# A masked copy as eight memory-to-memory transfers: the order in which two DMA queues go through the rows

## The chip, the cores and the metric

The kernel runs on one core of a Trainium2 chip. The metric is the device time of one launch in microseconds (us); a lower time is better. Of the core's engines only the two that issue the large transfers matter here, SyncE (SP) and ScalarE (ACT), with the 16 DMA engines that carry out what they issue. VectorE (DVE) and TensorE (PE) do a small test beside the transfers.

## The reference

```
batch, seq, hidden, capacity = 16, 1024, 512, 256
x: (16, 1024, 512) float32;  token_positions: (16, 1024) int, drawn from 0 to 255

mask = token_positions < capacity
return (x * mask[..., np.newaxis]).astype(np.float32)
```

A token whose position is at or beyond the capacity has its row of 512 numbers set to zero; every other row is returned as it is. With these inputs every position is below 256, so the output equals `x`.

## The kernel before, in words

The 16,384 rows of 2 KB are seen as 128 parts of 128 consecutive rows, one part for each partition number `p`. A part is 256 KB of consecutive memory, in `x` and in `out` alike, and part `p + 1` begins where part `p` ends. In the code `x_r` and `out_r` are this view, with the indices (p, n, d).

The kernel copies first and asks afterwards. Eight DMAs (L79) move `x` straight to `out` inside the device's memory, 4 MB each. DMA number `k` takes rows `k*16` to `k*16 + 15` of every part, which is block `k` of eight blocks of 32 KB in each of the 128 parts. The even `k` are issued by SP and the odd `k` by ACT, so each engine's queue holds four DMAs and works them off in the order of issue. All eight add to one semaphore, `s_copy`, and nothing waits between them. The list `early` gathers these DMAs, and a few lines of list handling move them to the front of the program, ahead of the start-up barrier of the engines. Ahead of ACT's four stands one small load (L72) of the positions to `tp`.

While the copies run, DVE builds the mask `keep` from `tp` in four operations (L103 to L115), sums it (L119), PE adds the sums over the partitions (L123), and DVE compares the total with the number of rows (L125). The answer, `drop_i`, says whether any token has to be dropped. SP, ACT and DVE read it and branch on it (L133, `nc.If(drop)`). Within the branch the kernel would load all rows to SBUF, multiply them by the mask and store them; with these inputs the branch isn't taken. At the end GpSimd (POOL) waits until `s_copy` has all eight DMAs, sets the semaphores back, and the program is over.

So the end of the program is set by the DMA that lands last. The order in which the blocks are copied is fixed by the loop over `k` and by the two queues, and no other step of the program reads what they write.

Of the kernel before, what the change touches and what calls it, by code (L numbers as in the profile page):

```python
# [1 line left out]

# [4 lines left out]


@with_exitstack
def kernel(  # L10
    ctx: ExitStack,
    tc: tile.TileContext,
    x: bass.AP,
    token_positions: bass.AP,
    capacity: bass.AP,
    out: bass.AP,
):
    nc = tc.nc
    P = nc.NUM_PARTITIONS
    fp32 = mybir.dt.float32  # L20
    i32 = mybir.dt.int32
    Alu = mybir.AluOpType

    x_f = x.flatten_outer_dims()
    out_f = out.flatten_outer_dims()
    N, D = x_f.shape
    n_per_p = N // P
    cap = float(int(capacity))
    x_r = x_f.rearrange("(p n) d -> p n d", p=P)
    out_r = out_f.rearrange("(p n) d -> p n d", p=P)  # L30
    tp_i32 = token_positions.rearrange("b s -> (b s)").bitcast(i32)

    sp = nc.sync
    act = nc.scalar
    ve = nc.vector
    pe = nc.tensor
    gp = nc.gpsimd


    tc.close()  # L40
    tc.compile()  # L41

    def sbuf(name, shape, dtype):
        return ctx.enter_context(nc.sbuf_tensor(name, shape, dtype)).ap()

    tp = sbuf("tp", [P, 2 * n_per_p], i32)
    ge = sbuf("ge", [P, n_per_p], fp32)
    lt = sbuf("lt", [P, n_per_p], fp32)
    low = sbuf("low", [P, n_per_p], fp32)
    keep = sbuf("keep", [P, n_per_p], fp32)  # L50
    kept = sbuf("kept", [P, 1], fp32)
    ones = sbuf("ones", [P, 1], fp32)
    drop_i = sbuf("drop_i", [1, 1], i32)
    total = ctx.enter_context(nc.psum_tensor("total", [1, 1], fp32)).ap()
    F = 16
    NBUF = 2
    n_fix = n_per_p // F
    xts = [sbuf(f"xt{b}", [P, F, D], fp32) for b in range(NBUF)]

    s_copy = nc.alloc_semaphore("s_copy")  # L60
    s_tp = nc.alloc_semaphore("s_tp")
    s_ve = nc.alloc_semaphore("s_ve")
    s_pe = nc.alloc_semaphore("s_pe")
    s_ld = [nc.alloc_semaphore(f"s_ld{b}") for b in range(NBUF)]
    s_mul = nc.alloc_semaphore("s_mul")
    s_st = [nc.alloc_semaphore(f"s_st{b}") for b in range(NBUF)]
    s_done = nc.alloc_semaphore("s_done")

    n_copy = 0
    early = []  # L70

    load_tp = act.dma_start(out=tp, in_=tp_i32.rearrange("(p w) -> p w", p=P))  # L72
    early.append(load_tp.then_inc(s_tp, 16).ins)

    C = 16
    for k in range(n_per_p // C):
        ins = (sp, act)[k % 2].dma_start(  # L79
            out=out_r[:, k * C : (k + 1) * C, :], in_=x_r[:, k * C : (k + 1) * C, :]  # L80
        ).then_inc(s_copy, 16)
        early.append(ins.ins)
        n_copy += 1


    home = nc.cur_bb.bb
    first_bb = nc.cur_f.blocks[0]
    first_sp = next(
        k for k, i in enumerate(first_bb.instructions) if i.engine == mybir.EngineType.SP
    )  # L90
    names = [i.name for i in early]
    home.instructions = [i for i in home.instructions if i.name not in names]
    first_bb.instructions = (
        first_bb.instructions[:first_sp] + early + first_bb.instructions[first_sp:]
    )

    lo = tp[:, 0 : 2 * n_per_p : 2]
    hi = tp[:, 1 : 2 * n_per_p : 2]


    ve.memset(ones, 1.0).then_inc(s_ve, 1)  # L101
    ve.wait_ge(s_tp, 16)
    ve.tensor_scalar(  # L103
        out=ge, in0=lo, scalar1=0.0, scalar2=None, op0=Alu.is_ge
    ).then_inc(s_ve, 1)
    ve.wait_ge(s_ve, 2)
    ve.scalar_tensor_tensor(  # L107
        out=lt, in0=lo, scalar=cap, in1=ge, op0=Alu.is_lt, op1=Alu.mult
    ).then_inc(s_ve, 1)
    ve.wait_ge(s_ve, 3)  # L110
    ve.scalar_tensor_tensor(  # L111
        out=low, in0=hi, scalar=0.0, in1=lt, op0=Alu.is_equal, op1=Alu.mult
    ).then_inc(s_ve, 1)
    ve.wait_ge(s_ve, 4)
    ve.scalar_tensor_tensor(  # L115
        out=keep, in0=hi, scalar=0.0, in1=low, op0=Alu.is_lt, op1=Alu.add
    ).then_inc(s_ve, 1)
    ve.wait_ge(s_ve, 5)
    ve.tensor_reduce(  # L119
        out=kept, in_=keep, axis=mybir.AxisListType.X, op=Alu.add  # L120
    ).then_inc(s_ve, 1)
    pe.wait_ge(s_ve, 6)
    pe.matmul(out=total, lhsT=ones, rhs=kept, start=True, stop=True).then_inc(s_pe, 1)  # L123
    ve.wait_ge(s_pe, 1)
    ve.tensor_scalar(  # L125
        out=drop_i, in0=total, scalar1=float(N) - 0.5, scalar2=None, op0=Alu.is_lt
    ).then_inc(s_ve, 1)


    for e in (sp, act, ve):  # L130
        e.wait_ge(s_ve, 7)
    ET = mybir.EngineType
    drop = nc.values_load(  # L133
        drop_i[0:1, 0:1],
        engines=[ET.SP, ET.Activation, ET.DVE],
        min_val=0,
        max_val=1,
        skip_runtime_bounds_check_because="a comparison gives 0 or 1",
    )
    with nc.If(drop):  # L140
        for u in range(n_fix):
            b = u % NBUF
            if u >= NBUF:
                sp.wait_ge(s_st[b], 16 * (u // NBUF))
            sp.dma_start(out=xts[b], in_=x_r[:, u * F : (u + 1) * F, :]).then_inc(s_ld[b], 16)
            ve.wait_ge(s_ld[b], 16 * (u // NBUF + 1))
            for j in range(F):
                c = u * F + j
                ve.tensor_scalar(
                    out=xts[b][:, j, :],  # L150
                    in0=xts[b][:, j, :],
                    scalar1=keep[:, c : c + 1],
                    scalar2=None,
                    op0=Alu.mult,
                ).then_inc(s_mul, 1)
            if u == 0:
                act.wait_ge(s_copy, 16 * n_copy)
            act.wait_ge(s_mul, (u + 1) * F)
            act.dma_start(out=out_r[:, u * F : (u + 1) * F, :], in_=xts[b]).then_inc(s_st[b], 16)
        for b in range(NBUF):  # L160
            act.wait_ge(s_st[b], 16 * (n_fix // NBUF))


    for e in (sp, act, ve):
        e.sem_inc(s_done, 1)
    gp.wait_ge(s_done, 3)
    own = [s_tp, s_ve, s_pe, *s_ld, s_mul, *s_st, s_done]
    ids = sorted(s.num for s in own)
    assert ids == list(range(ids[0], ids[-1] + 1))
    gp.sem_clear(range(ids[0], ids[-1] + 1))  # L170
    gp.wait_ge(s_copy, 16 * n_copy)
    gp.sem_inc(s_copy, -16 * n_copy)


# [1 line left out]
_INS = ['x', 'token_positions', 'capacity']  # L176
_OUTS = [((16, 1024, 512), 'float32')]

_NUMBERS = {'capacity': 256}


# [26 lines left out]
```

## Time and profile before

| | |
|---|---|
| median of 3 runs | 106.08 us (105.78 to 106.34) |
| the profiled execution, its own time | 106.19 us |
| its span, first to last instruction | 104.3 us |
| memory read, memory written | 33.69 MB, 33.55 MB |
| mean rate of the DMA engines over the span | 323 GB/s |
| DVE busy, PE busy | 1.5 us, 0.2 us |

The profile is of one execution, and its times count from the first instruction. Its DMA row is the mean busy share of the 16 DMA engines in 40 equal slices of the span, in tenths, and the row below it is what they moved. A copy from memory to memory counts once in that rate, and twice (read and written) in the memory's own line. `q1` and `q10` are the queues that SP and ACT fill. A packet is the piece that one DMA engine moves at a time. A window's rate counts each packet whole, so a short window is rough by a packet or two on each engine.

### The profile page before, as it was taken

The page shows a single profiled execution, that of the slowest core. Times are in us where ns is not written, and L with a number is a line of the kernel's source. Part 1 is how long each engine was busy: PE and PEld are TensorE (multiplying, and loading weights), DVE is VectorE, ACT ScalarE, POOL GpSimd, SP SyncE. Part 2 cuts the span into 40 slices and gives each one's busy share as a digit, 9 for nine tenths or more (in the row PEclk, how much of TensorE's full clock was granted, in tenths as well). Part 3 has the DMA queues.
Part 4 walks back from the last instruction along what each step waited for, and adds up shares of the span by engine and source line. Part 5 has one row for each costly group of instructions (what it writes and reads, how often), then busy time and mean ns, then how long its engine had stood idle before and what let it go on. Part 6 is the DMA issues. An engine that isn't in the chain of part 4 may idle for free. (4 is left out here: it accounts for less than half of the span.)

```text
span 104.3 us, 70 instructions
## 1 busy us (share of the span) xinstructions
PE 0.2 (0%) x2; PEld 0.1 (0%) x2; DVE 1.5 (1%) x7; POOL 0.2 (0%) x4
## 2 busy tenths in 40 slices
PE   0000000000000000000000000000000000000000
PEld 0000000000000000000000000000000000000000
DVE  0230000000000000000000000000000000000000
POOL 0000000000000000000000000000000000000000
DMA  8999989989989989999899997998997999989984
GB/s 251 402 352 302 339 280 339 339 302 352 339 289 390 314 276 377 289 327 352 289 364 327 302 377 239 377 377 289 352 327 276 377 327 314 390 276 327 364 277 163
DMA packets 1297, 33.69 MB, mean 323 GB/s; under 512 B 144, under 2 KB 272, under 8 KB 272
## 3 DMA queue, kind: packets, MB, share of 16 engines
q10 hardware_dynamic: 720, 16.91, 49.4%
q1 hardware_dynamic: 576, 16.78, 48.6%
q14 instruction: 1, 0.01, 0.0%
HBM read 33.69 MB, written 33.55 MB: 645 GB/s over the span
## 5 line engine op out<-in xcount | busy, mean ns | idle before, releaser
L107 DVE SCALAR_TENSOR_TENSOR lt<-tp,ge 128x128 f32<-128x128 int32 x1 | 0.3, 293 | 0.0
L111 DVE SCALAR_TENSOR_TENSOR low<-tp,lt 128x128 f32<-128x128 int32 x1 | 0.3, 291 | 0.0
L115 DVE SCALAR_TENSOR_TENSOR keep<-tp,low 128x128 f32<-128x128 int32 x1 | 0.3, 291 | 0.0
L119 DVE TENSOR_REDUCE kept<-keep 128x1 f32<-128x128 f32 x1 | 0.3, 286 | 0.0
L103 DVE TENSOR_SCALAR ge<-tp 128x128 f32<-128x128 int32 x1 | 0.2, 228 | 0.0
L123 PE MATMUL total<-kept,ones 128*1 128x1 f32 x2 | 0.2, 164 | 6.2 <-DVE kept L119 6.2
L125 DVE TENSOR_SCALAR drop_i<-total 1x1 int32<-1x1 f32 x1 | 0.1, 145 | 0.3 <-PE total L123 0.3
L101 DVE MEMSET ones<- 128x1 f32 x1 | 0.1, 59 | 4.6 <-PEq L41 4.6
L189 POOL MEMSET const-bfloat16-1.0<- 128x1 bf16 x1 | 0.1, 101 | 0.0
L189 POOL MEMSET const-uint8-127<- 128x1 uint8 x1 | 0.1, 101 | 0.0
L189 POOL MEMSET const-float32-0.0<- 128x1 f32 x1 | 0.1, 98 | 0.2 <-issue 0.2
L189 POOL MEMSET const-float32-1.0<- 128x1 f32 x1 | 0.1, 98 | 0.0
L123 PEld LDWEIGHTS total<-kept,ones 128*1 128x1 f32 x2 | 0.1, 80 | 6.2 <-DVE kept L119 6.2
## 6 DMA issues: line engine op xcount, KB each, us to landing
out_dram<-in_x_dram SPq DMA_DIRECT2D x4, 4096.0 KB, 62.2
out_dram<-in_x_dram ACTq DMA_DIRECT2D x4, 4096.0 KB, 68.1
tp<-in_token_positions_dram ACTq DMA_DIRECT2D x1, 128.0 KB, 2.1
```

The source lines that it names most:

```text
L101: ve.memset(ones, 1.0).then_inc(s_ve, 1)
L103: ve.tensor_scalar(out=ge, in0=lo, scalar1=0.0, scalar2=None, op0=Alu.is_ge).then_inc(s_ve, 1)
L107: ve.scalar_tensor_tensor(out=lt, in0=lo, scalar=cap, in1=ge, op0=Alu.is_lt, op1=Alu.mult).then_inc(s_ve, 1)
L111: ve.scalar_tensor_tensor(out=low, in0=hi, scalar=0.0, in1=lt, op0=Alu.is_equal, op1=Alu.mult).then_inc(s_ve, 1)
L115: ve.scalar_tensor_tensor(out=keep, in0=hi, scalar=0.0, in1=low, op0=Alu.is_lt, op1=Alu.add).then_inc(s_ve, 1)
L119: ve.tensor_reduce(out=kept, in_=keep, axis=mybir.AxisListType.X, op=Alu.add).then_inc(s_ve, 1)
L123: pe.matmul(out=total, lhsT=ones, rhs=kept, start=True, stop=True).then_inc(s_pe, 1)
L125: ve.tensor_scalar(out=drop_i, in0=total, scalar1=float(N) - 0.5, scalar2=None, op0=Alu.is_lt).then_inc(s_ve, 1)
L189: nc = _bacc.Bacc("TRN2", target_bir_lowering=False, num_devices=1)
```

## The change

The eight DMAs stay as they are in size, number, issuing engine and order of issue; the block that each takes is another. SP's four take blocks 0, 1, 2, 3 instead of 0, 2, 4, 6. ACT's four take blocks 7, 6, 5, 4 instead of 1, 3, 5, 7. Everything after the loop stands two lines lower and is unchanged.

```diff
     C = 16
-    for k in range(n_per_p // C):
+    n = n_per_p // C
+    for k in range(n):
+        j = k // 2 if k % 2 == 0 else n - 1 - k // 2
         ins = (sp, act)[k % 2].dma_start(
-            out=out_r[:, k * C : (k + 1) * C, :], in_=x_r[:, k * C : (k + 1) * C, :]
+            out=out_r[:, j * C : (j + 1) * C, :], in_=x_r[:, j * C : (j + 1) * C, :]
         ).then_inc(s_copy, 16)
         early.append(ins.ins)
         n_copy += 1
```

## The prediction

> **What bounds the kernel now.** I read the page first, since the chain of waits holds nothing but the mask (DVE 2%) and so can't say what the rest of the span is. The answer is in the rows for the DMA engines.
>
> ```profile
> span 104.3 us, 70 instructions
> ...
> DMA  8999989989989989999899997998997999989984
> ...
> DMA packets 1297, 33.69 MB, mean 323 GB/s; under 512 B 144, under 2 KB 272, under 8 KB 272
> ## 3 DMA queue, kind: packets, MB, share of 16 engines
> q10 hardware_dynamic: 720, 16.91, 49.4%
> q1 hardware_dynamic: 576, 16.78, 48.6%
> ...
> HBM read 33.69 MB, written 33.55 MB: 645 GB/s over the span
> ```
>
> The 16 DMA engines are busy from end to end, 49.4 + 48.6 = 98.0% of the span, and the two queues have equal shares. Of 1297 packets 272 are small ones and one is program code; the other 1024 are the copy, 8 DMAs x 128 parts, one packet for each 32 KB block of a part. So each engine moves 64 of them, in 0.980 x 104.3 = 102.2 us, or 1.60 us each.
>
> Next, when the queues work and which one ends last, from the issues and the landings:
>
> ```profile
> 0.00 2.94 SPq L79 DMA_DIRECT2D out_dram<-in_x_dram  x4
> ...
> 0.56 2.70 ACTq L79 DMA_DIRECT2D out_dram<-in_x_dram  x4
> ```
>
> ```profile
> out_dram<-in_x_dram SPq DMA_DIRECT2D x4, 4096.0 KB, 62.2
> out_dram<-in_x_dram ACTq DMA_DIRECT2D x4, 4096.0 KB, 68.1
> ...
> DMA to landing us min/median/max: 25.0/65.2/101.7
> ```
>
> All eight are issued within 3.3 us, and then nothing is issued again: the engines work off two full queues. SP's first lands 25.0 us after its issue. SP's median, 62.2 + about 1.2 for the issue = 63.4, lies between its second and third, so one DMA follows another every (63.4 - 25.0) / 1.5 = 25.6 us, at about 25, 51, 76 and 102 us. ACT's stand 6.3 us later (68.1 + 1.6 = 69.7), and the last of all lands at 101.7 + 2.5 = 104.2 us, 0.1 us before the end of the span. Two queues of equal share, 8 packets per engine in each DMA: 16 x 1.60 = 25.6 us, the same number.
>
> So SP and ACT share the engines packet by packet already, and SP is ahead by 6.3 / 3.2 = 2 packets on every engine. When SP reaches its next block, ACT is still finishing the one before for 6 us. Windows cut at the landings set those stretches apart:
>
> ```profile
> 3.30:5.90 2.60, 0.00 (x0) 0.00 (x0) 1.12 (x6) 0.00 (x0) 1.00 1.05 416
> 5.90:25.10 19.20, 0.19 (x2) 0.09 (x2) 0.42 (x2) 0.00 (x0) 1.00 1.01 332
> 25.10:31.10 6.00, 0.00 (x0) 0.00 (x0) 0.00 (x0) 0.00 (x0) 1.00 0.98 328
> 31.10:50.40 19.30, 0.00 (x0) 0.00 (x0) 0.00 (x0) 0.00 (x0) 1.00 1.01 326
> 50.40:56.80 6.40, 0.00 (x0) 0.00 (x0) 0.00 (x0) 0.00 (x0) 1.00 0.98 328
> 56.80:76.00 19.20, 0.00 (x0) 0.00 (x0) 0.00 (x0) 0.00 (x0) 1.00 1.00 328
> 76.00:82.30 6.30, 0.00 (x0) 0.00 (x0) 0.00 (x0) 0.00 (x0) 1.00 1.02 333
> 82.30:101.30 19.00, 0.00 (x0) 0.00 (x0) 0.00 (x0) 0.00 (x0) 1.00 1.01 331
> ```
>
> The last column is GB/s. Four long stretches (SP and ACT on blocks 0 and 1, then 2 and 3, 4 and 5, 6 and 7) run at 332, 326, 328, 331; the three short ones (SP on 2, 4, 6 while ACT ends 1, 3, 5) at 328, 328, 333. The first row is the early time with mostly SP's packets in flight, at 416: the engines can move more than 329 for a moment, so the steady rate isn't set by their own pace alone but by the memory, which takes 2 x 329 = 658 GB/s then. That is the one resource on which an order of addresses could act.
>
> **The change part by part.** It removes and adds no instruction: 4 + 4 DMAs of 4096 KB stay on the same queues, in the same order of issue, behind the same load of `tp`. Their issue (2.94 and 2.70 us, some 0.6 us each) lies under the transfers; if a DMA took longer to issue, the next would have the 20 us and more in which a queue still works on the DMA ahead of it. Nothing is moved past another instruction on SP, ACT or POOL, there is no new wait, and the mask's 1.5 us of DVE and 0.2 us of PE end at 6.6 us, more than 95 us before the span does. Cost: 0.
>
> The packets stay 1024 of 32 KB, in the same 256 KB steps from part to part. SP's first DMA is the same block 0, so the start (1.5 us from issue to the first packets) is the same, and so is the landing at the end: the same queue, the same two packets behind. Cost: 0.
>
> What is changed is the addresses that are in flight together. Before, SP and ACT are in neighbouring blocks, 32 KB apart, in all four phases of 25.6 us; after, 7, 5, 3 and then 1 block apart (224, 160, 96, 32 KB). As SP is two parts ahead, 512 KB, the true distances are 512 - 32 = 480 KB before, and 288, 352, 416, 480 KB after. The last phase is as before, so at most 3 x 25.6 = 77 us can change at all. No view of before shows the new distances, so the cost is bounded from both sides.
>
> By the row: the nearest is the set of seven windows. In the short ones SP is one block above ACT's, in place of one below, and at the other end of the part, so the distance in memory is another (with ACT in its last rows and SP in its first, some 1.5 MB instead of 0.5). Weighted by length they run at 330, the long ones at 329. A short window holds about 62 packets, so two packets at its edge are 3%; over the three together it is about 2%. No trend with the block number either: 332 to 331. This says 0, within 2% of 77 us = 1.5 us either way.
>
> By the rule that speaks against the change: the Trainium skill, "DMA: Bandwidth & Descriptors", section "Latency and other measured facts", has memory-to-memory copies losing rate as the step between partitions grows by powers of two: 207 GB/s at 512 KiB where 214 is the full rate, worse from there, and a shift of 4 KiB brings it back; it supposes that streams fall on the same memory channels. Here the step is 256 KB and the copy runs at 329 GB/s, above its full rate, so its figures are another setting; and all distances above, old and new, are off a power of two by more than 4 KiB. Taken at its mildest price all the same, 207/214 makes 3.3% of 77 us = 2.5 us, an estimate from that page. By the row the sum is 104.3 + 0 + 1.89 (the execution's own 106.19 less its span) = 106.19; by the rule 108.7. I take the row: it is of this kernel and this memory, and the rule's own condition isn't met by the new distances more than by the old.
>
> For a gain there is a bound as well: the skill's "HBM Reference", section "Specifications (TRN2)", gives some 716 GB/s for the memory that a pair of cores shares. The 67.24 MB would take 93.9 us at that, against 645 GB/s over the span, so 9% is the most that any order could bring by it; the early 416 x 2 = 832 GB/s is above that page's figure, though, and that window is short. Going steadily at 658, the memory is already at 92% of it, which leaves a better order little and a worse one more.
>
> Sum: 106.19 + 0, against the median of 106.08, which is 0.11 lower; I forecast 106.1.
>
> **The rivals.** No effect: the queues still share the engines packet by packet, and the memory spreads either set of addresses as evenly. For it: seven windows within 1% of 329, whatever the block. Time: 106.1, 105.6 to 106.6; what a measurement of this kernel can tell from no change is about 0.5%, 0.53 us. Chance 0.50.
>
> Slower, by streams that collide: with the queues 288 to 416 KB apart, reads of one and writes of the other fall on the same parts of the memory more often. Place: the first three phases, 77 us; price: 0 to 3.3%, so up to 2.5 us and 108.6 from the median, with 107.4 in the middle; it decides when the rate there is lower than 329 by 0.7% (0.53 / 77). For it: the memory is near its limit, so any clash shows at once; the 1.60 us packet against the early ones at 416 / 16 = 26 GB/s (1.26 us) says that there are clashes already. Against it: the even windows. Chance 0.29.
>
> Faster, by fewer clashes: two neighbouring blocks worked on at once may be what costs part of that 1.60 us. Place: the same 77 us, and 1% (the spread from the mean to the best window, 333 against 329) makes 0.8 us: 105.3; 2% makes 104.6. Against it: the short windows have other neighbours and gain nothing that can be told. Chance 0.21.
>
> That the change doesn't do what it says is part of the first: "taking turns" goes on in the engines, and only the block numbers differ.
>
> **How the numbers follow.** Faster 0.21, same 0.50, slower 0.29. Both rivals' bounds are open, and the slower one reaches further. From 104.9 to 108.2 the range holds the whole first case, nearly three quarters of the faster one and six sevenths of the slower, about 0.88; I keep that, as the price of a clash is the least known.
>
> **What would show it.** In the profile after: q1 and q10 near 48.6 and 49.4%, 33.69 and 33.55 MB at 645 GB/s, SP's median landing near 62 us and ACT's near 68, the same windows at 326 to 333. Slower by clashes: the windows up to 76 us below 326 and the last, from 82 us, at 331 again, SP's median landing past 63. Faster: the same windows above 333, landings earlier. The forecast is wrong if the span moves by over 0.5 us; if it moves with all windows even, the last one too, then the distance between the queues isn't the reason.

## The result and the profile after

The changed kernel takes 106.11 us (median of 6 runs, 106.01 to 106.39) against 106.05 us (median of 6, 105.78 to 106.34) for the kernel before (the three runs of the table and three more): a ratio of 1.0013, 95% interval 0.9991 to 1.0035. No difference is shown. The forecast was 106.1, with no effect as the likeliest case at a chance of one half.

The profiled execution after was the slowest of its six, 106.39 us with a span of 104.5 us. Its page, the rows for the DMA engines and the memory:

```profile
span 104.5 us, 70 instructions
...
DMA packets 1297, 33.69 MB, mean 322 GB/s; under 512 B 144, under 2 KB 272, under 8 KB 272
...
q10 hardware_dynamic: 720, 16.91, 49.6%
q1 hardware_dynamic: 576, 16.78, 48.4%
...
HBM read 33.69 MB, written 33.55 MB: 643 GB/s over the span
```

Its issues (KB each and the median time from issue to landing), then the least, median and longest of the eight:

```profile
out_dram<-in_x_dram SPq DMA_DIRECT2D x4, 4096.0 KB, 62.4
out_dram<-in_x_dram ACTq DMA_DIRECT2D x4, 4096.0 KB, 68.4
...
DMA to landing us min/median/max: 25.1/65.4/102.0
```

The packets are the same, the shares of the queues are within 0.2 points, and the least, median and longest landing are within 0.3 us of where they were. The windows, cut at the same places (the last column is GB/s):

```profile
5.90:25.10 19.20, 0.19 (x2) 0.09 (x2) 0.42 (x2) 0.00 (x0) 1.00 1.02 332
25.10:31.10 6.00, 0.00 (x0) 0.00 (x0) 0.00 (x0) 0.00 (x0) 1.00 1.01 333
31.10:50.40 19.30, 0.00 (x0) 0.00 (x0) 0.00 (x0) 0.00 (x0) 1.00 0.99 326
50.40:56.80 6.40, 0.00 (x0) 0.00 (x0) 0.00 (x0) 0.00 (x0) 1.00 1.00 333
56.80:76.00 19.20, 0.00 (x0) 0.00 (x0) 0.00 (x0) 0.00 (x0) 1.00 1.00 326
76.00:82.30 6.30, 0.00 (x0) 0.00 (x0) 0.00 (x0) 0.00 (x0) 1.00 1.04 333
82.30:101.30 19.00, 0.00 (x0) 0.00 (x0) 0.00 (x0) 0.00 (x0) 1.00 0.99 329
```

With the queues 7 blocks apart (first row), 5 (third), 3 (fifth) and 1 (last) the four long stretches give 332, 326, 326, 329, against 332, 326, 328, 331 before, when all four were 1 block apart. The rate doesn't follow the distance, as far as windows can tell: the trace before, cut at whole microseconds instead, gives 320 to 350 for the same seven stretches. The time is the sharper figure, and it leaves at most 0.35% for the change.

That the time stands still doesn't yet say why. Either no relation between addresses in flight matters to this memory, or one does and the change left it alone. The experiments separate the two. Three forms of a stall were put up against theory A, that the memory takes every such order at some 658 GB/s of reads and writes: B, the distance between the two queues counts; C, two queues sharing the engines cost something; D (later F), the steps within one DMA, between the 16 engines, count. E asks whether the memory sets the packet's 1.60 us at all. What goes on inside the memory isn't recorded; "collision" below is a name for a loss that comes with certain addresses. Ratios are against the kernel before on the same chip, where its median was 104.95 to 105.13 us, 1% below the 106.05 above; they are formed from the single runs and can differ a little from the quotient of two medians. One run of the first experiment, 153.45 us, is more than 1.5% above the fastest of its kernel and is left out of the median and the ratio.

### The profile page after: what moved, and what is told of

It is laid out like the page before. It is cut to its first block, busy times and chain, and to the rows that moved or that the text cites. A ratio compares the mean times of both kernels' runs of the same rounds, so it can differ in the third digit from the quotient of the medians.

```text
span 104.5 us, 70 instructions
## 1 busy us (share of the span) xinstructions
PE 0.2 (0%) x2; PEld 0.1 (0%) x2; DVE 1.5 (1%) x7; POOL 0.2 (0%) x4
## 2 busy tenths in 40 slices
DMA packets 1297, 33.69 MB, mean 322 GB/s; under 512 B 144, under 2 KB 272, under 8 KB 272
## 3 DMA queue, kind: packets, MB, share of 16 engines
q10 hardware_dynamic: 720, 16.91, 49.6%
```

## Experiments on the queues

**Both queues in the same block.** With `xg` and `og` the rows seen as 16 groups of 8 parts, (g, h, n d):

```diff
-    for k in range(n_per_p // C):
+    for k in range(2 * (n_per_p // C)):
+        h = 4 * (k % 2)
+        c = slice((k // 2) * C * D, (k // 2 + 1) * C * D)
         ins = (sp, act)[k % 2].dma_start(
-            out=out_r[:, k * C : (k + 1) * C, :], in_=x_r[:, k * C : (k + 1) * C, :]
+            out=og[:, h : h + 4, c], in_=xg[:, h : h + 4, c]
         ).then_inc(s_copy, 16)
```

> SP copies parts 0 to 3 of each engine's eight, ACT parts 4 to 7, both in block 0, then 1, and so on: 16 DMAs of 2 MB, the same 1024 packets of 32 KB. The two queues are then a whole number of 256 KB parts apart, 512 KB when SP is two packets ahead, instead of some blocks of 32 KB off that. Theory A (the memory takes any such order at one rate, 658 GB/s of reads and writes): 106.1 us, within 0.5 us, windows at 326 to 333 GB/s. Rival B (the distance between the two queues counts, and old and new order happened to be alike): at least 3.3% of the 98 us of copying more, 109.3 us or above. The eight additional DMAs could add some tenths of a us.

Measured: 151.81 us against 105.01, ratio 1.4407 (1.4311 to 1.4503). Theory A falls: there is an order at which this memory is 44% slower. But the edit did two things. It put the queues into the same block, and it wrote the 16 groups as the outermost dimension, which puts the 16 engines 2 MB apart if each takes one group. The next two runs undo one of them each.

**The 2 MB step kept, the queues from the two ends.** ACT's blocks run from 7 down to 0, as in the change under study:

```diff
+        j = k // 2 if k % 2 == 0 else n - 1 - k // 2
-        c = slice((k // 2) * C * D, (k // 2 + 1) * C * D)
+        c = slice(j * C * D, (j + 1) * C * D)
```

> As the run with the same block (SP on parts 0 to 3 of each engine's eight, ACT on parts 4 to 7), but ACT takes the blocks from 7 down to 0, so that the queues are 7, 5, 3, 1 and then again 1, 3, 5, 7 blocks off a whole number of parts. Theory F (the 152 us came from the 2 MB step between the 16 engines within one DMA, whichever block the other queue is in): 150 to 154 us again. Rival B (it came from the two queues standing in the same block): about 106 us.

Measured: 151.55 us (one run). The block of the other queue makes no difference that could be told from the 150.28 to 153.45 us of the same-block runs.

**The same block kept, the 2 MB step gone.** SP on parts 0 to 63, ACT on 64 to 127, with the parts as the outermost dimension again (`H` is 64, `h` is 0 or 64, `j` is `k // 2`):

```diff
-            out=out_r[:, k * C : (k + 1) * C, :], in_=x_r[:, k * C : (k + 1) * C, :]
+            out=out_r[h : h + H, j * C : (j + 1) * C, :],
+            in_=x_r[h : h + H, j * C : (j + 1) * C, :],
```

> SP copies parts 0 to 63, ACT parts 64 to 127, both in block 0, then 1, and so on; the access is written as 64 parts by 32 KB, with the parts as the outermost dimension as before. The queues stand 16 MB less two or so parts apart, always in the same block. Theory F (only the steps within a DMA count): 105 us, within 1 us of the kernel before. Rival B: 109 us or above, up to the 152 us of the other same-block run.

Measured: 105.08 us against 105.13, ratio 1.0001 (0.998 to 1.0022). Rival B is out from both sides: queues in the same block run at full rate here, and queues in far blocks are as slow as near ones where the step is 2 MB. The 16 DMAs of 2 MB, in place of 8 of 4 MB, cost nothing either.

**One queue alone.** All eight DMAs by SP, `ins = sp.dma_start(...)`.

> All eight DMAs on SP's queue, blocks 0 to 7 in order; ACT only loads the positions. Theory A: no second queue is needed and none costs anything, packets stay at 1.60 us and the time at 106.1 us, within 1 us, SP's landings every 12.8 us. Rival C (two queues sharing the engines cost the difference between the early 416 GB/s and the later 329): the early rate goes on, 33.55 MB at 416 GB/s is 81 us and the whole about 85 us; anything below 104 us speaks for a part of that.

Measured: 105.19 us against 105.01, ratio 1.0017 (0.9998 to 1.0036). The windows of that run:

```profile
1.50:5.90 4.40, 0.00 (x0) 0.00 (x0) 0.00 (x0) 0.00 (x0) 1.00 1.16 418
5.90:20.00 14.10, 0.19 (x2) 0.09 (x2) 1.54 (x7) 0.00 (x0) 1.00 1.01 331
20.00:40.00 20.00, 0.00 (x0) 0.00 (x0) 0.00 (x0) 0.00 (x0) 1.00 1.00 334
```

The rate starts high and settles at 331 GB/s with no second queue there. So the high early rate is something of the start, and rival C is out. What ends it isn't shown by these runs. The 418 itself is too high: a window counts every packet that begins in it as whole, and at the start of a copy all 16 engines begin one. By the packets' records the first 64, four for each engine, went out over 5.6 us, which is 373 GB/s (364 in the kernel before). Only the second sixteen are as short as the 418 makes them, 1.33 us in the mean (1.23 before); the fourth sixteen take 1.50 (1.57 before).

**The 2 MB step on one queue.** The sixteen DMAs of the first experiment, all by SP.

> The sixteen DMAs of the run with the same block and the 2 MB step, all on SP's queue; no second queue stands anywhere. Theory F (the collisions are among the 16 engines within one queue's wave, 2 MB apart): 148 to 154 us, as with two queues. Rival B in its last form (it takes two queues in the same parts of the memory): near 105 us, or at least clearly below 140 us.

Measured: 149.54 us (one run). Its page:

```profile
span 147.7 us, 78 instructions
...
q1 hardware_dynamic: 1280, 33.56, 97.6%
...
HBM read 33.69 MB, written 33.55 MB: 455 GB/s over the span
```

Here 97.6% of 16 engines' 147.7 us for 1024 packets is 2.25 us each, against 1.60. The loss is within one queue's packets; a second queue isn't needed for it.

## Experiments on the steps within a DMA

**Half the engines.** The first experiment's form on 8 groups at a time (`a` is the half of the parts, `g` runs over 8), 32 DMAs of 1 MB:

```diff
+    xe = x_f.rearrange("(a g h n) d -> a g h (n d)", a=2, g=8, h=8)
...
+            out=oe[a][:, h : h + 4, c], in_=xe[a][:, h : h + 4, c]
```

> Only 8 of the 16 DMA engines copy, each twice the packets (128 of 32 KB): the first half of the parts, then the second, 32 DMAs of 1 MB, queues as in the run with the same block. Theory A (the memory sets the 1.60 us): with half the traffic a packet takes 1.21 to 1.26 us, so 128 x 1.24 = 159 us and 4 around it, some 160 to 166 us. Rival E (1.60 us is an engine's own pace in a copy from memory to memory): 128 x 1.60 = 205 us and 4 around it, some 209 us.

Measured: 160.78 us (one run). From its page:

```profile
DMA  5445544544554455455445545544554454455442
...
q10 hardware_dynamic: 784, 16.91, 24.8%
q1 hardware_dynamic: 640, 16.78, 24.8%
```

The DMA row at 4 and 5 tenths says that an outermost dimension of 8 keeps 8 engines at work, so this dimension does set how many engines work (the Trainium skill has that rule, "DMA: Bandwidth & Descriptors", section "Why a DMA increments its semaphore by 16 and not by 1"). And 49.6% of 16 x 158.9 us for 1024 packets is 1.23 us each: an engine's own pace. The 1.60 us of the kernel before is not that; it comes with 16 engines copying at once. Nor do 32 DMAs in place of 8 slow the packets.

**The step, from 32 KB to 2 MB.** In all four that follow, the outermost dimension is 16, taken to be one index for each engine, and its step is another each time. Two things change with it: the step from an engine's packet to its next within a DMA (in the table below), and from 512 KB up the number and size of the DMAs, which cost nothing in the runs with 64 parts and with 8 engines. For 256 KB (8 DMAs, blocks and queues as before; 32 KB has `"(t h g n) d -> t g h (n d)"` and one `t` for each DMA):

```diff
+    xi = x_f.rearrange("(h g n) d -> g h (n d)", g=16, h=8)
...
-            out=out_r[:, k * C : (k + 1) * C, :], in_=x_r[:, k * C : (k + 1) * C, :]
+            out=oi[:, :, c], in_=xi[:, :, c]
```

For 512 KB (16 DMAs; 1 MB has `a=2, h=4` and 32 DMAs):

```diff
+    xg = x_f.rearrange("(a g h n) d -> h g a (n d)", a=4, g=16, h=2)
...
+            out=og[h][:, :, c], in_=xg[h][:, :, c]
```

> Each DMA copies one consecutive stretch of 4 MB; the 16 engines take neighbouring 32 KB pieces, 32 KB apart in place of 2 MB, and then go on by 512 KB. Still eight DMAs of 4 MB and 1024 packets of 32 KB. Theory A: 106.1 us within 0.5 us. Rival D (the 2 MB steps between the 16 engines make them collide, which is why a packet takes 1.60 us and not 1.21 to 1.26): the rate goes up by several per cent, to 102 us or lower; the other sign, over 107 us, would also say that the layout counts and only the queues' distance does not.

> The kernel before in its blocks, its queues and its order, with the 16 engines as the outermost dimension: in one wave they take 16 neighbouring parts, 256 KB apart, and go on by 4 MB. Theory F (large steps between the engines cost, small ones don't): 104 to 107 us, as 32 KB steps gave 107.5. If the time is as before within 0.5 us, a step of 256 KB is as good as whatever the 128-part form does. Rival G (any power-of-two step written out in this way is bad): over 120 us.

> The 16 engines as the outermost dimension, 512 KB apart in one wave (SP on the even parts, ACT on the odd ones, both in the same block; 16 DMAs of 2 MB). Theory F graded (each doubling of the step puts more packets in flight on the same parts of the memory): between the 105.2 us of 256 KB and the 152 us of 2 MB, and near the 3% by which the row of the Trainium skill falls at 512 KiB (207 for 214 GB/s): some 108 us, an estimate from that. Rival H (all is well until 2 MB, where something else begins): 105 us within 1 us.

> The same with 1 MB between the engines (SP on parts 0 and 2 of each four, ACT on 1 and 3; 32 DMAs of 1 MB). Theory F graded: 112 to 130 us. Rival H: 105 us, within 1.5 us for the additional DMAs.

Measured, with the 2 MB run from above:

| step between engines | step within an engine | time, us | ratio to the kernel before |
|---|---|---|---|
| 32 KB | 512 KB | 107.52 | 1.0234 (1.0201 to 1.0267) |
| 256 KB | 4 MB | 105.21 | 1.0005 (0.9985 to 1.0024) |
| 512 KB | 8 MB | 106.39 | 1.0138 (1.0106 to 1.0171) |
| 1 MB | 16 MB | 112.51 | 1.0708 (1.0681 to 1.0736) |
| 2 MB | 256 KB | 151.81 | 1.4407 (1.4311 to 1.4503) |

From 256 KB up the loss grows with every doubling of the step between engines, as graded theory F has it. Rival H (nothing until 2 MB) is out, and so is rival G (any such step written out is bad), by the 105.21 us. The step within an engine was never varied alone. Over the five rows the loss doesn't follow it, and 8 engines with the 2 MB form's two steps lose nothing (1.23 us). But it grows along with the other from 256 KB to 1 MB, so the 1.4% and the 7% could in part be due to it. At 512 KB the loss is less than half of the 3% that was expected from the skill's row, and the 106.4 us is 1.6 us below the estimate. The miss is at the other end: rival D expected a gain from 32 KB, 102 us or lower, and it is 2.3% slower instead. The layout counts there too, but these runs don't show why; a large step between engines can't be the reason.

**Pieces of 34 KB.** Seven DMAs of 128 pieces of 17 rows, one behind the other, and one with the rest:

```diff
+        rows = 17 if k < 7 else (N - done) // P
+        part = slice(done, done + P * rows)
+            out=out_f[part, :].rearrange("(p n) d -> p n d", p=P),
+            in_=x_f[part, :].rearrange("(p n) d -> p n d", p=P),
```

> Seven DMAs copy 128 pieces of 17 rows (34 KB), one behind the other, and the eighth what is left (128 pieces of 9 rows), so that no step between packets is a power of two; queues take turns as before. Theory F in its strong form (the 1.60 us packets of the kernel before still hold collisions by power-of-two steps): below 104 us. Theory A (658 GB/s is what the memory gives to any order that is spread well): 105 us, within 1 us.

Measured: 105.94 us against 105.13, ratio 1.0078 (1.005 to 1.0106). Its page, then the queues of the 256 KB run on the same chip (span 103.2 us):

```profile
span 103.9 us, 70 instructions
...
DMA packets 1217, 33.69 MB, mean 324 GB/s; under 512 B 144, under 2 KB 272, under 8 KB 272
...
q1 hardware_dynamic: 576, 17.83, 51.2%
q10 hardware_dynamic: 640, 15.86, 46.1%
```

```profile
q10 hardware_dynamic: 720, 16.91, 49.5%
q1 hardware_dynamic: 576, 16.78, 48.4%
```

For each 32 KB an engine takes 97.3% of 16 x 103.9 us by 1024, 1.58 us, and with the 256 KB step 97.9% of 16 x 103.2 by 1024, 1.58 as well. Steps that are no power of two gain nothing, so the 1.60 us isn't shown to hold collisions that such a step would remove. That is for theory A with the limit that the order is spread well. So the loss isn't in the packets. It is for the most part time in which engines have none: 2.7% of the span, 2.8 us, against 2.1%, 2.2 us. The page's 1217 packets are 80 fewer than the 1297 of the kernel before. In the trace the eighth DMA went as 48 packets of 48 KB, not as the 128 of 18 KB that the code writes, while the other seven have 128 of 34 KB each. Each of these DMAs is one consecutive stretch, so how it was shared out, and with it the step between the engines, isn't known in this run.

**One direction at a time.** Blocks 0 to 3 alone, through the core's on-chip memory SBUF (`held` are four tiles of 4 MB, `s_half` a new semaphore); blocks 4 to 7 are left out:

```diff
+            out=held[k], in_=x_r[:, k * C : (k + 1) * C, :]
+        ).then_inc(s_half, 16)
...
+    for e in (sp, act):
+        early.append(e.wait_ge(s_half, 64).ins)
...
+            out=out_r[:, k * C : (k + 1) * C, :], in_=held[k]
```

> Half of the work, blocks 0 to 3 alone, through SBUF and one direction at a time: four DMAs of 4 MB read them (their packets in the 256 KB steps of the kernel before), and when all have landed four write them; the other half of the output isn't written. Theory A (what holds the copy is reads and writes together, 658 GB/s): one direction alone is held by the engines' own pace, 1.21 us for 32 KB as with eight engines, 432 GB/s, so 39 us for each 16.8 MB and about 85 us in all. Rival E (an engine can't go below 1.60 us when all 16 work): 329 GB/s, 51 us each and about 108 us in all.

Measured: 84.83 us (one run). Its queues and its windows, reads up to 42 us and writes after:

```profile
q1 hardware_dynamic: 576, 16.78, 47.7%
q10 hardware_dynamic: 720, 16.91, 47.5%
```

```profile
5.90:20.00 14.10, 0.00 (x0) 0.00 (x0) 0.00 (x0) 0.00 (x0) 1.00 0.96 415
20.00:40.00 20.00, 0.00 (x0) 0.00 (x0) 0.00 (x0) 0.00 (x0) 1.00 1.03 446
40.00:45.00 5.00, 0.00 (x0) 0.00 (x0) 1.22 (x6) 0.00 (x0) 1.00 0.61 256
45.00:60.00 15.00, 0.19 (x2) 0.09 (x2) 0.32 (x2) 0.00 (x0) 1.00 1.02 437
60.00:80.00 20.00, 0.00 (x0) 0.00 (x0) 0.00 (x0) 0.00 (x0) 1.00 0.98 421
```

With all 16 engines at work, reads alone go at 415 to 446 GB/s and writes alone at 421 to 437. 95.2% of 16 x 82.9 us for 1024 packets is 1.23 us each, the pace of the eight engines. Rival E is out: 16 engines together do go at their own pace when the memory has one direction to serve. Read and write together, 2 x 329 = 658 GB/s, is where the copy is held. That the memory itself holds it, and not the way there, is argued from the loss at a 2 MB step, where only addresses differ; no run separates the two.

## Why the prediction was right

**The bound.** "The steady rate isn't set by their own pace alone but by the memory" is borne out from both sides: 8 engines, or 16 in one direction, take 1.23 us for a packet, and 16 engines copying take 1.60. The line it was read from is weaker than it looked. The 416 GB/s of the early window counts packets whole, and the packets' records give 364 over four packets of each engine; what carries the reading is the 1.23 us of the second sixteen packets.

**The parts costed at nothing.** Issue (2.93 and 2.70 us after, 2.94 and 2.70 before), packets, shares and the start are unchanged. The copying phases are too: all seven windows fall in the forecast 326 to 333.

**The addresses.** The row chosen, the windows of the kernel before, gave 0 within 1.5 us, and that held. But it is less even than it was said to be: "within 1% of 329" holds at the cuts chosen, and at whole microseconds the same trace gives 320 to 350. So the row bore the 0 only to within a few per cent; that the change came out at 0.1% and not at 1% is more than it could promise, and as far as the row goes it is luck. The reason behind the 0 is also not quite the one given. The first case said that the memory spreads either set of addresses as evenly, and the rivals asked which distance between the queues might collide. The memory doesn't spread every set of addresses evenly (44% at the 2 MB step). The runs show that the distance between the queues isn't a quantity that counts (one queue 1.0017, two in the same block 1.0001), while the steps within a DMA are, by up to 44%, with the step between the 16 engines as the likely one. The change leaves all steps within a DMA alone. So the list of distances, 480 KB against 288, 352, 416, 480 KB, priced the wrong relation, though the price taken was 0. It also rested on two packets' lead being two neighbouring parts, that is, on eight neighbouring parts for each engine. A packet's record doesn't name its address, so no trace shows that, and the runs speak against it: written out, that form takes 151.81 us and the kernel before 105.01.

**The rule weighed against the row.** The skill's rule on row pitch was set aside with two reasons. That its condition isn't met more by the new distances than by the old was right, but for a simpler reason: the rule is about the pitch within a transfer (the page infers streams in step with each other, and says that this isn't verified), and the change doesn't touch that. That "its figures are another setting" holds for their size. The page has 164 for 2 MiB where 214 is full, 30% more time; here 2 MB took 44% more, and 512 KB 1.4% where the page has 3.4%. Direction and growth are the page's, though its pitch is that between partitions and the step here is that of the outermost 16.

**The rivals.** "There are clashes already" in the 1.60 us, said for the slower case, has no support: 34 KB pieces (1.58) and one queue alone (97.9% of 16 x 103.8 us for 1024 packets, 1.59) leave it where it is, and it falls to 1.23 only when the traffic in the memory falls by a third or more. The faster rival's claim, that two neighbouring blocks at once cost something, is answered by the single queue: there the neighbour is gone and the time is the same. The gain that the page's 716 GB/s would leave is 10% of the span by the prediction's own figures (93.9 against 104.3 us), not 9%, and was reached by none of these orders: the highest rate over a span was 653 GB/s, in the run with 64 parts:

```profile
HBM read 33.69 MB, written 33.55 MB: 653 GB/s over the span
```

Two more sums are slightly off and change nothing: 214/207 is 3.4% more time, and the stated shares of the three cases inside the range add up to about 0.91, not 0.88.

## What to carry to other kernels

In a copy that keeps all 16 DMA engines busy, look at the steps of the access pattern within a DMA, above all at that of an outermost dimension of 16, before the order of the DMAs or their share between queues: here the order was worth no more than 0.35% and the steps up to 44%. When a change rearranges addresses, first write down which relation between packets in flight it changes, and test that relation alone; an experiment that changes two, as the first one here, needs one run for each. And when a profile shows one rate whatever block is at work, believe it for the relations that really vary between its windows, and cut the windows at other places once, to see how far the rate can be trusted.

## What the runs showed of the hardware

The copy before and after settles at 326 to 333 GB/s (some 658 GB/s of reads and writes), while reads or writes alone run at the engines' pace of 1.23 us for 32 KB. At a step of 2 MB, 16 engines settle at 211 to 236 GB/s, hardly more than the 213 to 221 of 8 engines at that step. Unexpected was the small loss at neighbouring pieces of 32 KB, 2.3%, and that the loss at 2 MB is there with one queue (149.54 us) as with two. Which engine takes which of 128 parts isn't shown by the traces, so which step the kernel before has isn't known; it runs as the written-out 256 KB.
